# An encoder step on one core: the feed forward's input product by seven quarter products instead of eight

## The chip, the core and the metric

The kernel runs on one core of a Trainium2 chip. Its metric is the device time of one execution in microseconds (us). Five engines run their own queues, each in the order of the program: TensorE (PE in the profile, its weight loads PEld), VectorE (DVE), ScalarE (ACT), GpSimd (POOL), and SyncE (SP), which starts most transfers from memory.

## The reference

One step of a four-layer encoder for 512 prompt rows and 32 sample rows, model width 1024. Each layer has a token mixer (differential attention, mLSTM, latent attention, differential attention) and then a SwiGLU feed forward of 2816 hidden features, both behind a norm whose scale and shift come from a conditioning vector. All is computed in fp32. The part that matters here:

```python
def swiglu(h, w_in, w_out):
    a, b = jnp.split(h @ w_in, 2, axis=-1)
    return (jax.nn.silu(a) * b) @ w_out
...
        mod = (jax.nn.silu(c) @ p['w_ada'][i] + p['b_ada'][i])[:, None, :]
        sh1, sc1, gt1, sh2, sc2, gt2 = jnp.split(mod, 6, axis=-1)
...
        h = rmsnorm(x, p['g_norm2'][i]) * (1.0 + sc2) + sh2
        x = x + gt2 * swiglu(h, p['w_ffn_in'][i], p['w_ffn_out'][i])
```

## The kernel before

Activations lie transposed, 128 features to a tile and all 544 rows side by side, in two halves of 256 and 288 rows (`HALVES`). Every fp32 product is three products of a faster format: each operand is split into a high part (ScalarE's cast, `hi`) and a low part (a subtraction, `lo`), and high x high, low x high and high x low are summed in a bank of PSUM (`prod`). `split(hi, lo, src, eng)` does this; the subtraction runs on VectorE, for a few weights on GpSimd (`ON_POOL`). In the profile a weight is `raw` as loaded, `wh` and `low` when split.

The feed forward (`ffn`) has 22 column tiles `t`, each with a weight of 128x1024 for `a` and one for `b`, 8 K tiles of 128 each. For a tile, both halves of the rows are multiplied with both weights, 2 x 2 x 8 x 3 matmuls, and `glu` makes silu(a) * b (`uf`) and splits it into `uh` and `ul`. After 11 tiles an output block (`out_block`) multiplies them with the output weights, 8 output tiles in two halves, and VectorE adds each to the residual `x` (`residual`). Then come the other 11 tiles and their output block, with the squares for the next norm (`ss`, on GpSimd).

The conditioning (`mod`) of the next layers is not TensorE's work: `ada_dve` loads 128x1024 of its weights at a time (`ada`) and VectorE multiplies and sums them with the conditioning (`sc`), once for the prompt and once for the sample. It is done during the feed forwards of the first three layers, in time that VectorE has left.

`Sched` sets the order of all work ahead of time, from the author's estimate of what each instruction takes (`Engine.cost`, `Tensor._held`): an instruction takes the first free time of its engine after its operands (`hole`), work given to `later` fills the rest (`fill`), and each engine's instructions are issued in the order of the estimated times. The estimate counts each engine's time by itself. On the chip each engine then runs its queue in that order and waits where an operand is late. All recorded instructions have one line, 296 (VectorE, ScalarE, GpSimd) or 329 and 332 (TensorE), so that the rows are told apart by their tiles.

Of the kernel before, what the change touches and what calls it, by code (L numbers as in the profile page):

```python
# [8 lines left out]
F32 = mybir.dt.float32  # L9
# [6 lines left out]
P = 128  # L16
D = 1024
# [14 lines left out]
HALVES = ((0, 256), (256, T))  # L32
# [19 lines left out]
def EARLY(h, z):  # L52
    """How many of the first conditioning's tiles are made after a projection."""
    return 0 if h == 0 else 2 if z == 2 and h < 4 else 1


class Sched:
    """An order of all engines' work, from an estimate of when each instruction can run.

    Tasks are generators that issue the tensor engine's work; each yields when its next step can start: None or a  # L60
    function that gives the time. The other engines' instructions take the first free time after their operands.
    Instructions are noted first and issued by their time, a phase at once.
    """
# [49 lines left out]
    def flush(self):  # L113
        """Issues what is noted, in the order of its time."""
# [13 lines left out]
    # what is known of a tile: (first and last partition, first and last column, time)  # L128
# [42 lines left out]
    def free(self, key, bufs):  # L171
        """When a new tile of a ring can be written."""
# [3 lines left out]
    def ready(self, *aps):  # L176
        """When the tensor engine can read."""
# [9 lines left out]
    def hole(self, eng, t, cost, take=True):  # L187
        """The first free time of an engine, from t on."""
# [59 lines left out]

class Engine:
    """An engine whose instructions are noted with their time."""  # L250
# [50 lines left out]
class Tensor:  # L301
    """The tensor engine, with an estimate of how long it is held."""
# [4 lines left out]
    def _held(self, out, lhs, rhs, passes, issue, turn=False):  # L307
# [8 lines left out]
        else:  # L316
            cost = max(passes * m / 2400.0, m / 1200.0, passes * n / 2400.0) + 0.0025
# [9 lines left out]
    def matmul(self, out, lhsT, rhs, start, stop):  # L327
        self._held(out, lhsT, rhs, 1 if lhsT.dtype == F32R else 4,
                   lambda: self.pe.matmul(out, lhsT, rhs, start=start, stop=stop))  # L329
# [6 lines left out]
def tile_trunk(ctx: ExitStack, tc: tile.TileContext, I, O):  # L336
# [31 lines left out]
    class Banks:  # L368
        """PSUM banks for products and turned tiles, each use in the one that is free first.

        A bank for turned tiles is written and read before another one is asked for; one for products is shut.
        """

        def __init__(self, n):
            self.last, self.shut = [None] * n, [True] * n
# [2030 lines left out]
```

## Time and profile before

| | |
|---|---|
| median of 3 runs | 2750.12 us (2749.83 to 2750.35) |
| profiled execution | span 2748.0 us from the first to the last instruction, 2.1 us under the median; its own time outside the span isn't given |
| TensorE | busy 2705.6 us, 98% |
| VectorE | busy 1820.7 us, 66% |
| ScalarE | busy 1086.5 us, 40% |
| GpSimd | busy 238.0 us, 9% |
| mean granted TensorE clock | 0.996 of full |

Busy time is what an engine spent in instructions, waits inside an instruction with it. Shares over the span mix stages; a stage is read from a window. A matmul's duration in a row is longer than the time to the next one's start, because matmuls overlap; their rate is read from starts.

### The profile page before, as it was taken

The page shows a single profiled execution, that of the slowest core. Times are in us where ns is not written, and L with a number is a line of the kernel's source. Part 1 is how long each engine was busy: PE and PEld are TensorE (multiplying, and loading weights), DVE is VectorE, ACT ScalarE, POOL GpSimd, SP SyncE. Part 2 cuts the span into 40 slices and gives each one's busy share as a digit, 9 for nine tenths or more (in the row PEclk, how much of TensorE's full clock was granted, in tenths as well). Part 3 has the DMA queues.
Part 4 walks back from the last instruction along what each step waited for, and adds up shares of the span by engine and source line. Part 5 has one row for each costly group of instructions (what it writes and reads, how often), then busy time and mean ns, then how long its engine had stood idle before and what let it go on. Part 6 is the DMA issues. An engine that isn't in the chain of part 4 may idle for free.

```text
span 2748.0 us, 51869 instructions
## 1 busy us (share of the span) xinstructions
PE 2705.6 (98%) x21223; PEld 2590.8 (94%) x21223; DVE 1820.7 (66%) x3621; ACT 1086.5 (40%) x2382; POOL 238.0 (9%) x242
## 2 busy tenths in 40 slices
PE   9999999999999999999999999999999999999998
PEld 6888899999999999999998899999998899999998
DVE  6878777777665677777366767777558887433333
ACT  4555442122466442223255534222235554321222
POOL 1000300000200120000110020000031112000001
PEclk9999999999999999999999999999999999999999
DMA  8343244555222235455221124555333222222221
GB/s 281 129 139 123 87 153 164 187 172 180 87 83 78 76 110 174 170 183 176 80 97 33 47 78 142 170 181 177 126 108 97 77 80 75 77 88 90 88 86 68
DMA packets 101461, 330.94 MB, mean 120 GB/s; under 512 B 12840, under 2 KB 20140, under 8 KB 100840
## 3 DMA queue, kind: packets, MB, share of 16 engines
q1 hardware_dynamic: 95976, 309.48, 33.6%
q0 software_dynamic: 5248, 18.14, 1.8%
q8 instruction: 167, 2.74, 0.4%
q14 instruction: 70, 0.57, 0.1%
HBM read 314.69 MB, written 12.89 MB: 119 GB/s over the span
## 4 chain that ended last, share of the span: by engine, by line
PE 90%; DVE 6%; ACT 2%; issue 1%; DMA 0%; DVEq 0%; SPq 0%; ACTq 0%
PE mm L329 54%; PE S L329 21%; PE O L329 11%; PE T L329 2%; PE T L332 2%; DVE ht L296 1%; DVE hl L296 1%; DVE x L296 1%; ACT hh L296 1%; ACT wh L296 0%; DVE low L296 0%; DVE rq L296 0%; DVE mx L296 0%; DVE ql L296 0%; ACT rs L296 0%
## 5 line engine op out<-in xcount | busy, mean ns | idle before, releaser
L329 PE MATMUL mm<-hh,wh 128*128 128x288 f32 (+1 forms) x3078 | 909.8, 296 | 0.5 <-ACT hh L296 0.4
L329 PE MATMUL mm<-hh,low 128*128 128x288 f32 (+1 forms) x3078 | 887.9, 288 | 0.0
L329 PE MATMUL mm<-hl,wh 128*128 128x288 f32 (+1 forms) x3078 | 884.5, 287 | 2.2 <-DVE hl L296 2.2
L329 PEld LDWEIGHTS mm<-hh,wh 128*128 128x128 f32 x3078 | 580.7, 189 | 22.3 <-issue 15.1
L329 PEld LDWEIGHTS mm<-hl,wh 128*128 128x128 f32 x3078 | 581.8, 189 | 2.6 <-DVE hl L296 2.6
L329 PEld LDWEIGHTS mm<-hh,low 128*128 128x128 f32 x3078 | 581.1, 189 | 3.3 <-issue 2.4
L296 ACT CAST wh<-raw 128x1024 fp32r<-128x1024 f32 (+2 forms) x392 | 399.9, 1020 | 335.7 <-PE mm L329 159.4
L296 DVE TENSOR_TENSOR low<-raw,wh 128x1024 fp32r<-128x1024 f32 (+2 forms) x358 | 421.8, 1190 | 153.4 <-ACT wh L296 152.0
L329 PE MATMUL S<-hh,wh 128*128 128x288 f32 (+1 forms) x892 | 257.5, 289 | 0.5 <-ACT hh L296 0.5
L329 PE MATMUL S<-hl,wh 128*128 128x288 f32 (+1 forms) x892 | 256.6, 288 | 1.0 <-DVE rq L296 1.0
L329 PE MATMUL S<-hh,low 128*128 128x288 f32 (+1 forms) x892 | 257.3, 288 | 0.0
L329 PE MATMUL mm<-uh,wh 128*128 128x288 f32 (+1 forms) x836 | 241.3, 289 | 0.0
L329 PE MATMUL mm<-uh,low 128*128 128x288 f32 (+1 forms) x836 | 240.5, 288 | 0.0
L329 PE MATMUL mm<-ul,wh 128*128 128x288 f32 (+1 forms) x836 | 239.9, 287 | 0.0
L296 ACT CAST uh<-uf 128x256 fp32r<-128x256 f32 (+1 forms) x176 | 73.9, 420 | 406.1 <-DVE uf L296 405.9
L296 DVE SCALAR_TENSOR_TENSOR x<-mm,mod,x 128x256 f32<-128x256 f32 (+1 forms) x278 | 103.7, 399 | 163.3 <-PE mm L329 162.4
L296 POOL TENSOR_TENSOR ss<-ss,sq 128x256 f32<-128x256 f32 (+1 forms) x80 | 75.6, 945 | 1537.2 <-ACT sq L296 1536.9
L296 DVE CUSTOM_DVE_ANT_0 ada<-ada,sc,bada 128x1024 f32<-128x1024 f32 x152 | 194.7, 1281 | 2.6
L296 DVE CUSTOM_DVE_ANT_0 junk<-ada,sc,bada 128x1024 f32<-128x1024 f32 x152 | 194.5, 1280 | 1.0 <-DMA ada<-in_w_adaT 0.9
L329 PEld LDWEIGHTS S<-hh,wh 128*128 128x128 f32 x892 | 167.5, 188 | 2.8 <-issue 2.1
L329 PEld LDWEIGHTS S<-hl,wh 128*128 128x128 f32 x892 | 168.1, 189 | 1.8 <-DVE rq L296 1.3
L329 PEld LDWEIGHTS S<-hh,low 128*128 128x128 f32 x892 | 167.6, 188 | 0.0
(487 smaller groups left out, 5212.5 us busy)
## 6 DMA issues: line engine op xcount, KB each, us to landing
raw<-in_w_fin SPq DMA_DIRECT2D x176, 512.0 KB, 3.3
ada<-in_w_adaT SPq DMA_DIRECT2D x152, 512.0 KB, 4.5
raw<-in_w_fo SPq DMA_DIRECT2D x64, 512.0 KB, 3.3
raw<-in_w_qkv SPq DMA_DIRECT2D x45, 512.0 KB, 3.8
raw<-in_w_ada SPq DMA_DIRECT2D x24, 512.0 KB, 3.7
raw<-in_w_fl SPq DMA_DIRECT2D x32, 384.0 KB, 3.1
raw<-in_w_bh SPq DMA_DIRECT2D x24, 512.0 KB, 3.5
raw<-in_w_ao SPq DMA_DIRECT2D x16, 512.0 KB, 3.6
```

The source lines that it names most:

```text
L296: return s.work(self.kind, outs, ins, self.cost(name, args, kw, outs, ins), lambda: f(*args, **kw))
L329: lambda: self.pe.matmul(out, lhsT, rhs, start=start, stop=stop))
L332: self._held(out, in_, ident, 0, lambda: self.pe.transpose(out, in_, ident), True)
```

## The change

Both halves of the rows become 272 wide (`W`). For column tiles 2 to 21 of each layer, the weights `a` and `b` are taken as a 2 x 2 matrix of quarters (`a` and `b`, K tiles 0 to 3 and 4 to 7), the input as another (K tiles 0 to 3 and 4 to 7, first and second half of the rows), and the product is formed from seven quarter products instead of eight, with sums of quarters on both sides. Tiles 0 and 1 stay as they were (`PLAIN`).

- The weights' sums S1 to S4 are made by GpSimd (`Feed.sums`: four instructions of 128x512, one in place in `raw`, the others `st`). S1 and the second weight's right half are split as one weight; S2, S3, S4 are split apart (`Feed.quarter`, tiles `sh` and `sl`): the low part of S2 on VectorE, of S3 on GpSimd, of S4 on GpSimd for 20, 15, 15 and 0 of the 20 tiles of a layer.
- The input's sums T1 to T4 are made once a layer (`Norm.forms`).
- A tile is a task of its own (`pair_task`); results are added in PSUM, or in SBUF (`cmb`) by VectorE. The product of the two branches and both low parts `ul` are GpSimd's, for the last tile of a block VectorE's.
- There are four output blocks of 6, 6, 6 and 4 tiles, loaded in pieces; of the eight output weights 1, 4 and 6 are split by GpSimd. The last block takes all first halves before the second ones.
- Conditioning weights are loaded and summed in halves of 512 columns, 608 sums instead of 304 of twice the width.
- Three more PSUM banks serve the products in the feed forward. The estimate of a matmul's time is a little longer.

```diff
-HALVES = ((0, 256), (256, T))
+W = T // 2
+HALVES = ((0, W), (W, T))
+BLOCKS = ((0, 6), (6, 12), (12, 18), (18, 22))
+MOST = 6
+QUARTERS = 4
+OUT_ON_POOL = (1, 4, 6)
+PLAIN = 2
...
-            cost = max(passes * m / 2400.0, m / 1200.0, passes * n / 2400.0) + 0.0025
+            cost = max(passes * m / 2400.0, m / 1200.0, passes * n / 2265.0) + 0.005
...
-            for bi in range(2):
-                yield 10 * l + 2 + 2 * bi
-                for t in range(11 * bi, 11 * bi + 11):
-                    yield from (I["w_fin"][l, t, z] for z in range(2))
-                yield 10 * l + 3 + 2 * bi
-                for j in range(0, KT, 2):
-                    yield from (I["w_fo"][l, bi, j], I["w_fl"][l, bi, j // 2], I["w_fo"][l, bi, j + 1])
+            for bi, (t0, t1) in enumerate(BLOCKS):
+                yield 10 * l + 2
+                for t in range(t0, t1):
+                    for z in range(2):
+                        yield I["w_fin"][l, t, z] if t < PLAIN else (Pair(I["w_fin"][l, t, z], z, t % 4 < (4, 3, 3, 0)[l]), None)
+                yield 10 * l + 3
+                n = 1 if t1 - t0 > 4 else 2
+                for j in range(0, KT, n):
+                    yield (Pieces(l, t0, t1, range(j, j + n)), G if j in OUT_ON_POOL else V)
...
+        def sums(self, k):
+            if self.pool is None:
+                return False
+            p = self.pairs[k]
+            if not self.room():
+                return False
+            a, b = self.raws[k], self.raws[k + 1]
+            s2, s3, s4 = (sb(self.pool, [P, 512], "st", bufs=3) for _ in range(3))
+            p.update(s2=s2, s3=s3, s4=s4)
+            hi = self.hi(k, a)
+            S_.copy(hi, a)
+            G.tensor_tensor(out=s3, in0=a[:, :512], in1=b[:, :512], op=ALU.subtract)
+            G.tensor_tensor(out=b[:, :512], in0=b[:, :512], in1=b[:, 512:], op=ALU.add)
+            G.tensor_tensor(out=s2, in0=b[:, :512], in1=a[:, :512], op=ALU.subtract)
+            G.tensor_tensor(out=s4, in0=a[:, 512:], in1=s2, op=ALU.subtract)
+            lo = los[k % RAWS]
+            sub(lo, a, hi)
+            p.update(A11=(hi[:, :512], lo[:, :512]), A12=(hi[:, 512:], lo[:, 512:]))
+            return True
+
+        def second(self, k):
+            if not self.room():
+                return False
+            raw = self.raws[k + 1]
+            hi, lo = self.hi(k + 1, raw), los[(k + 1) % RAWS]
+            split(hi, lo, raw)
+            self.pairs[k].update(S1=(hi[:, :512], lo[:, :512]), A22=(hi[:, 512:], lo[:, 512:]))
+            return True
+
+        def quarter(self, k, name):
+            q = self.quarters
+            if len(q) >= QUARTERS and q[-QUARTERS] not in self.used:
+                return False
+            q.append((k, name))
+            p = self.pairs[k]
+            hi, lo = (sb(self.pool, [P, 512], t, F32R, bufs=QUARTERS) for t in ("sh", "sl"))
+            split(hi, lo, p[name.lower()], G if name == "S3" or name == "S4" and p["pool"] else V)
+            p[name] = (hi, lo)
+            return True
...
+            first = sb(pool, [P, 2], "ada1", bufs=2)
+            for c in (slice(0, D // 2), slice(D // 2, D)):
+                raw = sb(pool, [P, D // 2], "ada", bufs=3)
+                SP.dma_start(out=raw, in_=I["w_adaT"][l, t][:, c])
+                for s in range(2):
+                    yield "DVE", (raw,), 0.65
+                    V.tensor_tensor_reduce(
+                        out=junk if s == 0 else raw,
+                        in0=raw,
+                        in1=sc[:, s, c],
+                        scale=1.0,
+                        scalar=first[:, s : s + 1] if c.start else bada[:, l, t : t + 1],
+                        op0=ALU.mult,
+                        op1=ALU.add,
+                        accum_out=mods[l][:, t, s : s + 1] if c.start else first[:, s : s + 1],
+                    )
...
+        def forms(self, am, sh, tf, pf, f):
+
+            a, b = HALVES[1]
+            c = SEQ - a
+            h = KT // 2
+            tables(SILU, self.rstd(a, b))
+            for j in range(KT):
+                t = f[:, j]
+                for side, d, e in ((0, 0, c), (1, c, W)):
+                    at = stt(t[:, d:e], x[:, j, a + d : a + e], am[:, j, side : side + 1], self.rs[:, a + d : a + e], ALU.mult, ALU.mult)
+                    act(t[:, d:e], t[:, d:e], AF.Identity, bias=sh[:, j, side : side + 1])
+                split(hh[:, j, a:b], hl[:, j, a:b], t)
+                pending.discard((j, a))
+                yield lambda: at - PACE
+
+            def fold(n, k, t, eng):
+                split(tf[n][0][:, k], tf[n][1][:, k], t, eng)
+                pf.done(n, k)
+
+            for k in range(h):
+                t3, t2 = f[:, k], f[:, k + h]
+                G.tensor_tensor(out=t3, in0=t2, in1=t3, op=ALU.subtract)
+                add(t2, t3, hh[:, k, :a].bitcast(F32))
+                at = add(t2, t2, hl[:, k, :a].bitcast(F32))
+                fold("T3", k, t3, G)
+                t4 = t3
+                sub(t4, hh[:, k + h, :a].bitcast(F32), t2)
+                fold("T2", k, t2, V)
+                G.tensor_tensor(out=t4, in0=t4, in1=hl[:, k + h, :a].bitcast(F32), op=ALU.add)
+                fold("T4", k, t4, V)
+                yield lambda: at - PACE
+            yield pf.after(("plain",))
+            for k in range(h):
+                t1 = sb(nrm, [P, W], "ht", bufs=4)
+                sub(t1, hh[:, k, a:b].bitcast(F32), hh[:, k, :a].bitcast(F32))
+                add(t1, t1, hl[:, k, a:b].bitcast(F32))
+                sub(t1, t1, hl[:, k, :a].bitcast(F32))
+                split(hh[:, k, a:b], hl[:, k, a:b], t1)
+                pf.done("T1", k)
+
...
+            inputs = {n: tf[n] for n in tf}
+            inputs["T1"] = (hh[:, :h, W:], hl[:, :h, W:])
+            inputs["B22"] = (hh[:, h:, W:], hl[:, h:, W:])
+            inputs["B11"] = (hh[:, :h, :W], hl[:, :h, :W])
+            inputs["B21"] = (hh[:, h:, :W], hl[:, h:, :W])
...
+            def product(p, wn, xn, ps, start=True):
+                xs = inputs[xn]
+                yield lambda: 0.0 if wn in p else NEVER
+                w = p[wn]
+                for k in range(h):
+                    ww, xx = wk(w, k), (xs[0][:, k, :], xs[1][:, k, :])
+                    yield lambda: ready(xn, k)
+                    yield lambda: max(sched.writable(ps), sched.ready(*ww, *xx))
+                    kw = {} if start else {"skip_group_check": True}
+                    PE.matmul(ps, ww[0], xx[0], start=start and k == 0, stop=False, **kw)
+                    PE.matmul(ps, ww[1], xx[0], start=False, stop=False, **kw)
+                    PE.matmul(ps, ww[0], xx[1], start=False, stop=k == h - 1, **kw)
...
+            def eng(t):
+                return V if any(t == t1 - 1 for _, t1 in BLOCKS) else G
+
+            def part(t, i, f):
+                a, b = HALVES[i]
+                uh, ul = u[t]
+                S_.copy(uh[:, a:b], f)
+                eng(t).tensor_tensor(out=ul[:, a:b], in0=f, in1=uh[:, a:b], op=ALU.subtract)
+                pf.done("u", t, i)
...
+            def pair_task(t, p):
+                k = p["k"]
+
+                def bank():
+                    ps = yield from mm_bank()
+                    return ps, ps[:, :W]
+
+                xb, X = yield from bank()
+                yield from product(p, "A11", "B11", X)
+                s1 = sb(fp, [P, W], "cmb", bufs=6)
+                S_.copy(s1, X)
+                yb, Y = yield from bank()
+                yield from product(p, "A12", "B21", Y)
+                feed.drop_keys(k)
+                add(s1, s1, Y)
+                banks.done(yb)
+                act(s1, s1, AF.Silu)
+                yield from product(p, "S2", "T2", X, False)
+                feed.drop_keys((k, "S2"))
+                s2 = sb(fp, [P, W], "cmb", bufs=6)
+                S_.copy(s2, X)
+                gb, g = yield from bank()
+                yield from product(p, "S1", "T1", g)
+                b1 = sb(fp, [P, W], "cmb", bufs=6)
+                S_.copy(b1, g)
+                yield from product(p, "S3", "T3", X, False)
+                feed.drop_keys((k, "S3"))
+                add(b1, X, b1)
+                yield from product(p, "S4", "B22", g, False)
+                feed.drop_keys((k, "S4"))
+                add(s2, s2, g)
+                banks.done(gb)
+                last = act(s2, s2, AF.Silu)
+                eng(t).tensor_tensor(out=b1, in0=b1, in1=s2, op=ALU.mult)
+                part(t, 1, b1)
+                if t == FT - 1:
+                    tables(EXP_LN, last)
+                pf.done("late", t)
+                yield from product(p, "A22", "T4", X, False)
+                feed.drop_keys(k + 1)
+                mul(s1, X, s1)
+                banks.done(xb)
+                part(t, 0, s1)
+                live[0] -= 1
...
+                if bi < len(BLOCKS) - 1:
+                    yield from out_block(load, drop, parts, gt, mm_bank, BOTH, lead=4)
+                else:
+                    yield from out_block(load, drop, parts, gt, mm_bank, last_by_half(NBH), Norm(), finish, lead=4)
```

The engines' queues show it at three places. In GpSimd's queue of the kernel before, in the first layer, the end of the input of the feed forward (`hs`, `hl`: the sample rows) is followed directly by the squares of its last output block (`ss`):

```order
L296 TENSOR_TENSOR hs_4773<-hs_4773,rs_1002 128x256
L296 TENSOR_TENSOR hs_4773<-hs_4773,mod_97 128x256
L296 TENSOR_TENSOR hl<-hs_4773,hh 128x8x32
L296 TENSOR_TENSOR ss_5108<-ss_5108,sq_5114 128x256
L296 TENSOR_TENSOR ss_5108<-ss_5108,sq_5118 128x288
```

In the kernel after, GpSimd's queue in the second block of that feed forward, for one column tile (`st` and `raw` are sums of weights, `sl` low parts of S3 and S4, `cmb` the product of the branches, `ul` its low parts):

```order
L310 TENSOR_TENSOR sl_4979<-st_4965,sh_4978 128x512
L310 TENSOR_TENSOR sl_4984<-st_4966,sh_4983 128x512
L310 TENSOR_TENSOR st_4986<-raw_57,raw_58 128x512
L310 TENSOR_TENSOR raw_58<-raw_58 128x512
L310 TENSOR_TENSOR st_4985<-raw_58,raw_57 128x512
L310 TENSOR_TENSOR st_4987<-raw_57,st_4985 128x512
L310 TENSOR_TENSOR cmb_4982<-cmb_4982,cmb_4980 128x272
L310 TENSOR_TENSOR ul_4954<-cmb_4982,uh_4953 128x272
L310 TENSOR_TENSOR ul_4954<-cmb_4974,uh_4953 128x272
```

Nothing stood there before; these nine instructions now stand there once for each of the 20 column tiles, seven or eight of them in a block's last tile or where S4 is VectorE's.

VectorE's queue in the first layer's feed forward before, for one column tile: two low parts of weights, the branches' product and its low part for a half, the conditioning sums (`ISA`, with the read of the accumulator as an instruction of its own):

```order
L296 TENSOR_TENSOR low_68<-raw_62,wh_4813 128x1024
L296 TENSOR_TENSOR low_63<-raw_57,wh_4814 128x1024
L296 TENSOR_TENSOR uf_4818<-S_4816,silu_4817 128x256
L296 TENSOR_TENSOR ul_4755<-uf_4818,uh_4754 128x256
L296 ISA junk_4801,mod_97<-ada_4804,sc_4800,bada 128x1024
L296 ISA mod_97 128x1
L296 ISA ada_4804,mod_97<-ada_4804,sc_4800,bada 128x1024
```

And after, in a tile of the third block:

```order
L310 TENSOR_TENSOR low_66<-raw_60,wh_5175 128x1024
L310 TENSOR_TENSOR low_65<-raw_59,wh_5174 128x1024
L310 TENSOR_TENSOR sl_5177<-st_5171,sh_5176 128x512
L310 TENSOR_TENSOR cmb_5193<-mm_5183,cmb_5193 128x272
L310 ISA junk_4783,ada_1389_5190<-ada_5191,sc_4782,bada 128x512
L310 ISA ada_1389_5190 128x1
L310 TENSOR_TENSOR cmb_5189<-cmb_5189,mm_5192 128x272
L310 ISA ada_5191,ada_1389_5190<-ada_5191,sc_4782,bada 128x512
```

The two low parts stay, that of S2 (`sl`) and the sums with PSUM (`mm`) come in, and the conditioning sums are half as wide and twice as many.

TensorE's queue after, where one tile's third product ends and its fourth begins (S2 with T2, then S1 with T1, whose tile is in `hh` and `hl`):

```order
L343 MATMUL mm_5010<-T2h_4740,sh_4990 128x272
L343 MATMUL mm_5010<-T2h_4740,sl_4991 128x272
L343 MATMUL mm_5010<-T2l_4741,sh_4990 128x272
L343 MATMUL mm_5029<-hh,wh_4989 128x272
L343 MATMUL mm_5029<-hh,low_64 128x272
L343 MATMUL mm_5029<-hl,wh_4989 128x272
```

Each product is 12 such rows, a tile has seven of them, 84 rows where there were 96 of 256 or 288 columns; TensorE's whole queue has 19161 rows where it had 20122.

## Rows read from the trace of the kernel before

**Rows 1.** Page, busy us of each engine (share of the span) xinstructions

```profile
span 2748.0 us, 51869 instructions
PE 2705.6 (98%) x21223; PEld 2590.8 (94%) x21223; DVE 1820.7 (66%) x3621; ACT 1086.5 (40%) x2382; POOL 238.0 (9%) x242
```

**Rows 2.** Windows: us; PE, PEld, DVE, ACT, POOL busy (instructions); clock; DMA share, GB/s

```profile
345.00:730.00 385.00, 385.00 (x3074) 384.89 (x3074) 274.90 (x439) 112.49 (x182) 13.80 (x13) 1.00 0.48 162
412.41:484.71 72.30, 72.30 (x580) 72.30 (x579) 53.85 (x85) 19.27 (x32) 0.00 (x0) 1.00 0.49 165
```

**Rows 3.** Timeline, VectorE, steady tiles: start, us, instruction xcount, idle before

```profile
411.46 0.46 DVE L296 TENSOR_TENSOR uf<-mm,silu 128x288 f32<-128x288 f32 x1 [1.31 <-PE mm L329]
412.79 2.35 DVE L296 TENSOR_TENSOR low<-raw,wh 128x1024 fp32r<-128x1024 f32 x2
...
424.84 2.35 DVE L296 TENSOR_TENSOR low<-raw,wh 128x1024 fp32r<-128x1024 f32 x2
```

**Rows 4.** Timeline, GpSimd, 256 and 1024 columns

```profile
313.67 0.74 POOL L296 TENSOR_TENSOR ss<-ss,sq 128x256 f32<-128x256 f32 x1 [16.21 <-ACT sq L296]
...
980.80 2.39 POOL L296 TENSOR_TENSOR low<-raw,wh 128x1024 fp32r<-128x1024 f32 x1 [7.09 <-ACT wh L296]
```

**Rows 5.** Timeline, GpSimd and VectorE at three places where both work

```profile
285.25 2.37 POOL L296 TENSOR_TENSOR low<-raw,wh 128x1024 fp32r<-128x1024 f32 x1 [4.82 <-ACT wh L296]
285.33 1.26 DVE L296 SCALAR_TENSOR_TENSOR x<-mm,mod,x 128x256 f32<-128x256 f32 x3
...
691.14 1.22 DVE L296 TENSOR_TENSOR low<-raw,wh 128x1024 fp32r<-128x1024 f32 x1
691.34 1.61 POOL L296 TENSOR_TENSOR ss<-ss,sq 128x256 f32<-128x256 f32 x1 [343.11 <-ACT sq L296]
692.27 1.50 DVE L296 TENSOR_TENSOR low<-raw,wh 128x768 fp32r<-128x768 f32 x1
692.91 1.53 POOL L296 TENSOR_TENSOR ss<-ss,sq 128x288 f32<-128x288 f32 x1
...
940.44 2.39 POOL L296 TENSOR_TENSOR low<-raw,wh 128x1024 fp32r<-128x1024 f32 x1 [7.33 <-ACT wh L296]
940.50 2.34 DVE L296 TENSOR_TENSOR dd<-nd,dd 128x1 f32<-128x1 f32 x1
...
944.86 0.16 DVE L296 TENSOR_TENSOR dd<-nd,dd 128x1 f32<-128x1 f32 x1
```

**Rows 6.** Timeline, VectorE, conditioning sums and a low part of 256

```profile
408.86 1.28 DVE L296 CUSTOM_DVE_ANT_0 junk<-ada,sc,bada 128x1024 f32<-128x1024 f32 x1
410.06 0.08 DVE L296 DVE_READ_ACCUMULATOR2_ANT mod<- 128x1 f32 x1
...
418.03 0.43 DVE L296 TENSOR_TENSOR ul<-uf,uh 128x256 fp32r<-128x256 f32 x1 [0.47 <-ACT uh L296]
418.37 1.28 DVE L296 CUSTOM_DVE_ANT_0 junk<-ada,sc,bada 128x1024 f32<-128x1024 f32 x1
```

**Rows 7.** Timeline, TensorE, starts of the first and fourth layer's feed forward

```profile
342.85 0.72 PE L329 MATMUL T<-ss,ones_d 128*128 128x288 f32 x2 [3.18 <-DVE ss L296]
...
2339.49 1.30 PE L329 MATMUL T<-ss,ones_d 128*128 128x288 f32 x2 [3.19 <-DVE ss L296]
...
2341.77 0.41 PE L329 MATMUL mm<-hh,low 128*128 128x256 f32 x1
2341.98 0.41 PE L329 MATMUL mm<-hl,wh 128*128 128x256 f32 x1
```

**Rows 8.** Windows at the same two places, columns as in rows 2

```profile
340.00:344.00 4.00, 1.16 (x5) 0.98 (x6) 3.90 (x7) 2.18 (x4) 2.00 (x3) 1.00 0.17 25
2338.00:2342.00 4.00, 2.50 (x7) 1.96 (x8) 2.55 (x5) 1.91 (x5) 0.91 (x1) 0.53 0.00 0
```

**Rows 9.** Groups of ScalarE by shape: xcount, busy us, mean ns, idle before

```profile
L296 ACT CAST wh<-raw 128x1024 fp32r<-128x1024 f32 x348 | 363.7, 1045 | 292.6 <-PE mm L329 159.4 <-PE S L329 65.9 <-PE O L329 23.5
...
L296 ACT CAST uh<-uf 128x288 fp32r<-128x288 f32 x88 | 38.1, 433 | 186.6 <-DVE uf L296 186.6
```

More of the change, by code (lines that the diff above doesn't have):

```diff
@@ L396, in done @@
                     self.shut[self.last.index(t.tensor.name)] = True
-    banks = Banks(5)
+    banks = Banks((pB, f"b{i}") for i in range(5))
     def t_bank():
@@ L455, in add @@
     def add(out, a, b):
-        V.tensor_tensor(out=out, in0=a, in1=b, op=ALU.add)
+        return V.tensor_tensor(out=out, in0=a, in1=b, op=ALU.add)
     def stt(out, a, s, b, op0, op1):
@@ L529, in all_weights @@
                 continue
-            yield (w, G) if not isinstance(w, tuple) and (stage, i) in ON_POOL else w
+            if isinstance(w, tuple) and isinstance(w[0], Pair):
+                yield w[0]
+            else:
+                yield (w, G) if not isinstance(w, tuple) and (stage, i) in ON_POOL else w
             i += 1
@@ L581, in first, with room, hi, plain @@
             self.taken = n
-            return self.tiles[:]
+            return [self.tiles[k] for k in range(n)]
+        def room(self, n=1):
+            return all(len(self.his) + i < SPLITS or self.his[i - SPLITS] in self.used for i in range(n))
+        def hi(self, k, raw):
+            self.his.append(k)
+            return sb(wp, raw.shape, "wh", F32R, bufs=SPLITS)
+        def plain(self, k, eng):
+            if not self.room():
+                return False
+            raw = self.raws[k]
+            hi = self.hi(k, raw)
+            lo = los[k % RAWS][: raw.shape[0], : raw.shape[1]]
+            split(hi, lo, raw, eng)
+            self.tiles[k] = (hi, lo, k)
+            return True
@@ new lines, in load @@
+        def load(self, k):
+            ap = self.aps[k]
+            eng = V
+            if isinstance(ap, tuple):
+                ap, eng = ap
+            t = raws[k % RAWS][: ap.shape[0], : ap.shape[1]]
+            with sched.not_before(sched.let_go(t.tensor.name)):
+                for c, src in ap.parts if isinstance(ap, Pieces) else ((slice(0, t.shape[1]), ap.ap if isinstance(ap, Pair) else ap),):
+                    SP.dma_start(out=t[:, c], in_=src)
+            self.raws.append(t)
+            if isinstance(ap, Pair):
+                if ap.z == 0:
+                    self.pairs[k] = {"k": k, "pool": ap.pool}
+                else:
+                    self.steps += [(self.sums, k - 1), (self.second, k - 1)]
+                    self.steps += [(self.quarter, k - 1, n) for n in ("S2", "S3", "S4")]
+            elif eng is None:
+                self.tiles[k] = (t, None, k)
+            else:
+                self.steps.append((self.plain, k, eng))
@@ L612, in get @@
             self.more(0)
-            assert len(self.tiles) >= self.taken, "a weight that is held too long"
+            assert self.taken - 1 in self.tiles, "a weight that is held too long"
             w = self.tiles[self.taken - 1]
```

306 lines of the change are left out of this document (164 added, 142 removed).

## The prediction

> **What bounds the kernel now.** I read the page's busy table first: TensorE 98% of a span of 2748.0 us, VectorE 66%, GpSimd 9% [rows 1]. Then the stages, since that share is an average: over the first layer's feed forward and over six of its steady column tiles TensorE never stops, VectorE works three quarters of the time and GpSimd almost none [rows 2]. The period of a steady tile is read from VectorE, whose two weight splits return every 12.05 us [rows 3]. A tile issues 2 outputs x 8 K tiles x 3 products x 2 halves = 96 matmuls, so one costs 12.05/96 = 0.1255 us, half of them 256 and half 288 wide; one of 272 columns is the mean and costs the same. TensorE is the bound, and only because GpSimd and VectorE stay out of its way.
>
> **TensorE's saving.** Seven quarter products of 4 K tiles x 3 instead of eight are 84 matmuls, 10.54 us a tile. The order has 961 fewer PE rows. 20 tiles in each of 4 layers use the seven, so 80 x 12 x 0.1255 = -120.5 us. By layer the input stage is 22 x 12.05 = 265 us of TensorE before, and 2 x 12.05 + 20 x 10.54 = 235 us after. The output products stay at 8 x 2 x 22 x 3 = 1056 a layer, 132.5 us, in four blocks instead of two. Halves of 272 change no sum.
>
> **What GpSimd gets.** Its subtractions take 0.74 us for 256 columns and 2.39 for 1024 [rows 4], so by a line through both 0.77 for 272, 1.29 for 512 and 1.84 for 768. A tile gives it four sums and one or two low parts of 512, a product and two low parts of 272: 6 x 1.29 + 3 x 0.77 = 10.05 us, or 8.8 where S4 is VectorE's. That alone nearly fills the 10.54. For the input stage of a layer: 20 x 10.05, less 4 x 2.3 for the tiles that close a block, plus 16 x 0.77 for the sums of the input and the two plain tiles, 204 us in layer 0; 198 in layers 1 and 2 (five S4 fewer), 178 in layer 3 (none).
>
> **What VectorE gets beside it.** Instructions with both inputs in SBUF: two low parts of 1024 (1.14 us apart [rows 3]) and one of 512 (0.60, half of it) a tile, 2.9 us; with S4 3.5. With 4.2 us at the blocks' ends and about 24 at the start (in the order 4 x 1.14 and 60 of 32 to 272 columns, 0.33 on average, as the 0.34 of 256 [rows 6]) that is 86 us in layer 0, 89, 89 and 98. Then the conditioning sums. The order sets 156, 144 and 144 halves of 512 into the input stages of layers 0 to 2 (the other 164 into the output blocks). One of 1024 holds the engine 1.20 us [rows 6]; half of it, with a fixed part of 0.07 as in the subtractions (0.34 for 256, 1.14 for 1024), is 0.64. So 100, 92 and 92 us. ScalarE has two casts of 1.05, three of about half that and seven short ones of about 0.4 [rows 9], 6.6 us a tile, and stays hidden.
>
> **The two engines exclude each other.** This is the step on which the forecast rests. VectorE's subtraction of a 1-element column takes 0.16 us, but 2.34 when GpSimd has just begun 1024 columns, and ends as GpSimd ends [rows 5]. It holds the other way too: GpSimd's 256 columns take 1.61 instead of 0.74 behind VectorE's split. Three VectorE instructions that read PSUM and one SBUF tile run beside a GpSimd subtraction at their usual 0.4 each. So instructions with two SBUF inputs on VectorE and GpSimd's subtractions, which have them too, take turns: their times add up. Where four of them alternate, 691.14 to 694.44 [rows 5], they take 3.30 us where 1.14 + 0.74 + 0.87 + 0.80 = 3.55 would be the plain sum (the last two by the lines above), 7% less, since a fixed part overlaps.
>
> No conditioning sum ran beside GpSimd in the trace; I take it to be shut out as well, because both its tensors, the weights and the conditioning, are in SBUF, and each such pair that met GpSimd waited, whatever its operation or size. The Trainium skill says the same more generally ("SBUF — State Buffer", section "Who interferes with whom"): a VectorE instruction with two SBUF inputs contends with a GpSimd instruction that reads SBUF, and the later one waits for the whole of the other. The trace agrees for the subtractions (2.34 us against 0.16); for these sums no run here shows it, and by the page alone they would be in the sum below.
>
> **The sum.** Taking turns, the input stage costs 204 + 86 + 100 = 390 us in layer 0, 198 + 89 + 92 = 379 in layers 1 and 2, 178 + 98 = 276 in layer 3. Some of it is done in the output blocks before: ten GpSimd instructions of 512 (12.9 us) and 1.4 us of VectorE stand there in the order, three times a layer, -43 us. Such a block then holds about 34 us of turns in 36 us of matmuls, so it still fits, with its doubled residual adds (24 instructions, 7.7 us). That leaves 347, 336, 336 and 233 us, against 235 of TensorE and 265 before: +82, +71, +71, and -30 in layer 3, where TensorE stays the bound. Together +194 us. To this I add 0.5 us a tile in layers 0 to 2, +30 us. GpSimd's queue is in order, and its product and low parts behind a tile need VectorE's last product (0.46) and ScalarE's cast (0.43) [rows 3, 9] first; the next tile's sums stand behind them. On the profiled execution's 2748.0 us, which lies 2.1 under the median of the runs, this gives 2972; on the median **2975 us**.
>
> Bounds of this case: below, turns 7% cheaper in layers 0 to 2, -80, and no waits, 2865. Above, the work ahead in the output blocks worth nothing, +129, and 1 us of waits more a tile, 3135. Costed at nothing: the split conditioning loads and the weights in pieces (same bytes; DMA is half busy [rows 2]), and the borrowed banks. The start of a feed forward already holds a TensorE wait of 3.2 us [rows 7]; the new input sums lie under 24 us of plain products, and their turns are in the sum.
>
> **Rivals.**
> 1. *TensorE stays the bound and all the new work is hidden*, not slower: 2750 - 120 + 0 to 10 us, 2630 to 2640. GpSimd's 10.0 us alone would fit under 10.54, and VectorE's too. It needs the two to run side by side, against all of rows 5. It decides if the turns of a tile fall under 10.5 us. Chance 6%.
> 2. *The conditioning sums don't take turns*, only the splits do: 290, 287 and 287 less 43, so 247, 244 and 244 against 265, and -30 in layer 3: 2750 - 18 - 21 - 21 - 30 = 2660. But VectorE alone then has 2.9 + 4 x 0.37 + 7.8 x 0.72 = 10 us a tile (0.72 with the 0.08 read of the accumulator [rows 6]), and waits up to three times 1.29 behind GpSimd, which brings a tile to 12 and more and the time back to 2750, or 2790 with waits in every tile. Middle 2710. Chance 15%.
> 3. *The clock falls in the new waits*, slower still. In layer 3 TensorE waited 3.19 us; the granted clock was 0.53 in the stretch after it (the lower of its levels, 1.2 GHz), and matmuls came 0.21 us apart [rows 7, 8], instead of the 0.12 of these 256 columns. In layer 0 a wait of 3.18 left it at full [rows 7, 8]. Turns of 17 us against 10.5 of matmuls leave 6 us a tile to wait. If that comes in one piece, each tile of layers 0 to 2 loses more: at 0.09 a matmul some 20 of them, about 2 us, 60 x 2 = +120: 3095, and 3150 to 3250 with the upper bound above. The Trainium skill ("TensorE: Matmul & The Clock Gate", section on HAM oscillation) tells of a kernel that falls to the low clock at every K tile because each waits for its load. One trace row agrees (0.53 after 3.19 us) and one does not (3.18 us in layer 0); by that rule the time would be the 3095 and more given here. Chance of a time over 3135: 9%.
> 4. *The change does not do what it says*: the order shows the 961 rows gone and the sums on GpSimd; excluded.
>
> **How the numbers follow.** The likeliest case, turns with the conditioning in them, has 70% and its own range 2865 to 3135. To leave out no more than 2 in 10 the range reaches down into rival 2 and a little into rival 3: 2690 to 3150. A measurement of this kernel tells 0.2%, 5.5 us, from no change. Faster: rival 1 whole and most of rival 2, 6 + 12 = 18%. Same: 3%, out of rival 2. Slower: 79%.
>
> **What would show it.** Right: in the input stages of layers 0 to 2 a period of 16 to 18 us a tile instead of 12.05; VectorE's splits of 1024 columns well over their 1.22 us and GpSimd's of 512 over 1.29, while VectorE's instructions on PSUM stay at 0.4; TensorE waiting for the high and low parts of the sums (sh, sl, wh, low), its busy share far under 98%; layer 3 the shortest of the four, near 10.5 to 12 us a tile; output blocks still at 36 us. Wrong: splits and GpSimd's sums at their old durations with TensorE over 95% busy (rival 1), conditioning sums at half of 1.28 us beside a running GpSimd (rival 2), or matmuls 0.21 us apart through the input stages (rival 3).

## The result and the profile after

The changed kernel takes 3017.75 us (median of 4 runs, 3016.6 to 3019.76) where the kernel before takes 2749.97: ratio 1.0972, 95% interval 1.0957 to 1.0988. It is 268 us slower. The forecast was 2975, its range 2690 to 3150.

The page of the changed kernel, which answers to [rows 1] (busy us of each engine, then PE's granted clock by fortieths of the span):

```profile
span 3014.8 us, 53523 instructions
PE 2722.9 (90%) x20258; PEld 2561.5 (85%) x20258; DVE 2458.2 (82%) x4711; ACT 1335.5 (44%) x3002; POOL 1315.0 (44%) x976
PEclk9999989989999998999999998989999999899999
```

TensorE has 965 matmul rows fewer and is no longer busy all the time; VectorE went from 66 to 82%, GpSimd from 9 to 44%.

To see where, I cut both traces into feed forwards (from the first matmul of the norm's sum to the last output matmul; in layer 0 after, 324.94 to 824.54 us) and the stretches between them:

| us, layers 0, 1, 2, 3 | feed forward | mixer ahead of it |
|---|---|---|
| before | 413.7, 415.5, 413.7, 416.3 | 322.5, 239.8, 238.7, 275.2 |
| after | 499.6, 483.5, 480.8, 430.2 | 324.9, 251.3, 243.3, 288.8 |
| difference | +85.9, +68.0, +67.1, +13.9 | +2.4, +11.5, +4.6, +13.6 |

The feed forwards lost 235 us and the mixers, which the change was not to touch, 32. Inside a feed forward, windows of the changed kernel (us; PE, PEld, DVE, ACT, POOL busy with instructions; clock; DMA share, GB/s), for [rows 2]: layer 0's first six tiles (from 344.00; their first input product starts at 348.4, behind a TensorE wait of 5.4 us), its second six, the output block between them, and six of layer 3.

```profile
344.00:440.20 96.20, 74.96 (x496) 70.50 (x497) 83.31 (x137) 49.11 (x105) 63.98 (x51) 0.84 0.27 87
476.19:565.16 88.97, 72.76 (x507) 70.23 (x506) 87.39 (x133) 34.32 (x68) 69.44 (x46) 0.92 0.39 126
440.22:476.19 35.97, 35.97 (x289) 35.97 (x288) 35.03 (x71) 8.80 (x12) 15.04 (x9) 1.00 0.59 187
2716.12:2787.47 71.35, 66.51 (x507) 65.28 (x506) 39.92 (x49) 33.15 (x66) 51.76 (x38) 0.98 0.26 80
```

Six tiles hold the predicted 504 matmuls, 63.2 us of them at [rows 3]'s rate, and take 89. VectorE is the engine without a gap there (87.39 of 88.97 us), but more than a third of that is waiting inside instructions: its own work in the window is some 56 us, an estimate from 46 us of instructions with two SBUF inputs, as added up further down, and 28 short ones that read PSUM, about 0.35 us each. The timelines of VectorE and of GpSimd in that stretch show it, as [rows 5] did for splits (start, duration, instruction):

```profile
519.69 1.26 DVE L310 CUSTOM_DVE_ANT_0 ada<-ada,sc,bada 128x512 f32<-128x512 f32 x1
520.88 0.08 DVE L310 DVE_READ_ACCUMULATOR2_ANT ada<- 128x1 f32 x1
520.88 0.43 DVE L310 TENSOR_TENSOR cmb<-mm,cmb 128x272 f32<-128x272 f32 x1
521.24 1.40 DVE L310 CUSTOM_DVE_ANT_0 junk<-ada,sc,ada 128x512 f32<-128x512 f32 x1
522.57 0.08 DVE L310 DVE_READ_ACCUMULATOR2_ANT mod<- 128x1 f32 x1
522.57 0.43 DVE L310 TENSOR_TENSOR cmb<-cmb,mm 128x272 f32<-128x272 f32 x1
522.92 1.42 DVE L310 CUSTOM_DVE_ANT_0 ada<-ada,sc,ada 128x512 f32<-128x512 f32 x1
```

```profile
520.37 3.42 POOL L310 TENSOR_TENSOR sl<-st,sh 128x512 fp32r<-128x512 f32 x2
523.74 1.75 POOL L310 TENSOR_TENSOR st<-raw,raw 128x512 f32<-128x512 f32 x1
```

Each conditioning sum (CUSTOM) takes 1.26 to 1.42 us, each low part on GpSimd 1.71, where the undisturbed times are 0.74 and 1.26 (run 5 below); the additions from PSUM (cmb, mm) keep their 0.43. [rows 6] had 1.28 us for a sum of twice the width.

### The profile page after: what moved, and what is told of

Its sections match the earlier page's. It is cut to its first block, busy times and chain, and to the rows that moved or that the text cites. A ratio compares the mean times of both kernels' runs of the same rounds, so it can differ in the third digit from the quotient of the medians.

```text
span 3014.8 us, 53523 instructions
## 1 busy us (share of the span) xinstructions
PE 2722.9 (90%) x20258; PEld 2561.5 (85%) x20258; DVE 2458.2 (82%) x4711; ACT 1335.5 (44%) x3002; POOL 1315.0 (44%) x976
## 5 line engine op out<-in xcount | busy, mean ns | idle before, releaser
L343 PE MATMUL mm<-hh,wh 128*128 128x272 f32 x2694 | 813.4, 302 | 35.5 <-ACT hh L310 25.7
L343 PE MATMUL mm<-hh,low 128*128 128x272 f32 x2694 | 789.3, 293 | 12.9 <-DVE low L310 12.9
L343 PE MATMUL mm<-hl,wh 128*128 128x272 f32 x2694 | 791.0, 294 | 9.7 <-DVE hl L310 9.6
L343 PE MATMUL mm<-uh,wh 128*128 128x272 f32 x1408 | 407.7, 290 | 6.9 <-DVE x L310 6.4
L343 PE MATMUL mm<-ul,wh 128*128 128x272 f32 x1408 | 408.2, 290 | 1.6 <-DVE ul L310 1.6
L343 PE MATMUL mm<-uh,low 128*128 128x272 f32 x1408 | 406.7, 289 | 0.0
L310 POOL TENSOR_TENSOR st<-raw,raw 128x512 f32<-128x512 f32 x160 | 250.1, 1563 | 98.2 <-DMA raw<-in_w_fin 33.1
L343 PEld LDWEIGHTS mm<-uh,wh 128*128 128x128 f32 x1408 | 266.6, 189 | 8.0 <-DVE x L310 6.9
L343 PEld LDWEIGHTS mm<-ul,wh 128*128 128x128 f32 x1408 | 266.1, 189 | 2.1 <-DVE ul L310 2.0
L343 PEld LDWEIGHTS mm<-uh,low 128*128 128x128 f32 x1408 | 266.5, 189 | 0.2
```

The lines of the kernel that those rows point to most:

```text
L310: return s.work(self.kind, outs, ins, self.cost(name, args, kw, outs, ins), lambda: f(*args, **kw))
```

## The experiments

Theory: instructions with two SBUF inputs on VectorE and GpSimd's take turns, and this sum of turns is the new bound of layers 0 to 2. First rival: VectorE is simply overloaded. Second: conditioning only fills gaps. The mixers' 32 us had no theory yet.

**1. S3 and S4 on VectorE.** One line of `quarter`:

```diff
-            split(hi, lo, p[name.lower()], G if name == "S3" or name == "S4" and p["pool"] else V)
+            split(hi, lo, p[name.lower()], V)
```

> The changed kernel with the low parts of S3 and S4 (130 of 512 columns, 110 of them in layers 0 to 2) all on VectorE; everything else as it is. Turn-taking (both engines share one order of turns): each move swaps a turn of about 1.29 us on GpSimd for one of about 0.60 on VectorE, so 130 x 0.69 = -90 us: 2928, between 2900 and 2960, and VectorE stays near 98% busy in the stages of layers 0 to 2 with fewer microseconds in each instruction. Rival, VectorE's own load is the bound there (98% busy) and GpSimd only runs beside it: 110 x 0.60 = +66 us more on the bound: 3084, between 3065 and 3100.

Measured: 2981.22 us, 36 less than the change, above the expected range. VectorE got 110 x 0.60 = 66 us more of its own work in layers 0 to 2, and their feed forwards still came out 23.5 us shorter together (494.9, 472.9 and 472.6), so overload falls. The blocks of six tiles went from 87 to 90 us to 81.5 to 82.2 in layers 0 to 2: 5.3 to 8.1 us less, where 10.5 to 12 moves a block make 7.2 to 8.3 by the theory. That agreement is in part luck: the planner also put fewer conditioning sums into these blocks, 33 instead of 43 in layer 0's second (477.99 to 560.17), 6.7 us less at 0.67 each. VectorE's own work in that block hardly changed, and the turns, added up as further down, fell by 15 us, the block by 7. In layer 3 the blocks went from 71.4 and 72.5 to 64.3 and 65.0. In all, the input blocks gained 76 us, and 41 were given back: 33 in the last output blocks of layers 0 to 2 and 8 in the mixers. Windows of this kernel (layer 0's second block and its last output block, and six tiles of layer 3):

```profile
477.99:560.17 82.18, 67.42 (x508) 65.44 (x506) 79.78 (x124) 35.46 (x68) 47.88 (x35) 0.98 0.39 122
769.36:824.08 54.72, 33.41 (x197) 30.85 (x196) 52.66 (x138) 10.21 (x19) 4.99 (x6) 0.72 0.51 162
2698.41:2762.69 64.28, 64.11 (x507) 63.66 (x506) 44.50 (x54) 33.49 (x66) 42.82 (x33) 1.00 0.30 89
```

The program, which knows nothing of turns, puts conditioning that found no gap ahead of the last output block (`fill(True)`). VectorE is full there, and the block took 54.7 us instead of 35.2. Layer 3 has no conditioning, and TensorE became its bound.

**2. No conditioning sums.** A constant stands in for the later layers' conditioning.

```diff
+            if queue:
+                V.memset(mods[l + 1], 0.1)
...
+                queue = []
             yield from ffn(l, after_ffn, queue, keep)
```

> The changed kernel without the conditioning sums and their loads (the conditioning of the later layers is a constant, so the output is not the reference's). Turn-taking with the conditioning in it: the stages of layers 0 to 2 fall from 87 to 90 us to about layer 3's 71 to 73, and a little more where S4 is GpSimd's; their feed forwards from 500, 484 and 481 us to 435 to 450: about -140, so 2878, between 2850 and 2910, and GpSimd's sums of 512 columns fall from 1.57 us towards 1.3. Rival, the conditioning only fills time in which VectorE waits, and the weight sums and splits alone make the loss: 3005 to 3018.

Measured: 2817.99 us, 200 less. Feed forwards 422.9, 425.8, 425.1 and 428.5; blocks of six 69.3 to 70.0 in layers 0 to 2; GpSimd's sums of two raw weights 1.375 us instead of 1.563. Layer 0's second block (columns as above):

```profile
468.12:537.54 69.42, 65.67 (x508) 63.92 (x507) 35.63 (x44) 34.14 (x67) 57.27 (x44) 1.00 0.28 82
```

The second rival falls. The time lies under the expected range: layers 0 to 2 came out a little under layer 3's 428.5, where 435 to 450 was expected. It also shows what stays: without any conditioning the change is still 2.4% slower than before (interval 1.0225 to 1.0255).

**3. Two sources of the mixers' 32 us, each alone on the kernel before.**

```diff
-HALVES = ((0, 256), (256, T))
+W = T // 2
+HALVES = ((0, W), (W, T))
```

> The kernel before with halves of 272 columns instead of 256 and 288, and nothing else of the change. Of the 32 us that the stages outside the feed forwards lost, the refitted estimate alone gave back 13.1 in layer 3's attention, but only 1.8 of the 11.5 in the mLSTM. If the halves make the mLSTM's loss (tiles of 128 rows now straddle their edge): 2760 to 2775. If the loss comes with the feed forward before it: 2747 to 2755.

Measured: 2761.07 us, ratio 1.0040 (1.0027 to 1.0053), but not in the mixers (323.7, 240.9, 238.1, 276.5): 8.2 of the 10 us lie in the first feed forward, most of them in its last output block. The time fell into the range given for the mLSTM, but the mLSTM lost only 1.1 us: the expectation named the wrong place.

```diff
-            cost = max(passes * m / 2400.0, m / 1200.0, passes * n / 2400.0) + 0.0025
+            cost = max(passes * m / 2400.0, m / 1200.0, passes * n / 2265.0) + 0.005
```

> The kernel before with the refitted estimate of a matmul (columns / 2265 + 0.005 instead of / 2400 + 0.0025), and nothing else of the change. It changes only the order in which instructions are written. If it is the cause of the 32 us outside the feed forwards: 2770 to 2785. If not: 2745 to 2755.

Measured: 2777.1 us, ratio 1.0095 (1.0080 to 1.0110). Mixers 325.8, 241.7, 239.6 and 288.4: layer 3's attention alone lost 13.2 of the 13.6 us, by the order of instructions and nothing else. How its rows stand differently there was not followed further.

**4. The changed kernel with the old estimate**, the same line the other way.

> The changed kernel with the old estimate of a matmul (columns / 2400 + 0.0025). If the estimate costs the same on both kernels (26 us on the kernel before): 2992, between 2985 and 3002. Rival, the new feed forward needs the refitted estimate to be ordered well, and what the mixers gain is lost there: 3010 to 3040.

Measured: 2968.95 us, 49 less, nearly twice what was expected: 18 in the mixers (324.5, 247.4, 240.6, 277.6) and 29 in the feed forwards (492.5, 478.0, 478.1, 416.4). The rival falls; the refitted estimate made the new feed forward worse too.

**5. The conditioning vector in PSUM.** The sharpest test of turns: the same sums, once with both inputs in SBUF, once with one in a PSUM bank.

```diff
+            if l and at != (s, c):
+                S_.copy(by, sc[:, s, c])
+                at = s, c
...
-                in1=sc[:, s, c],
+                in1=by if l else sc[:, s, c],
```

> Control for the next run: the changed kernel with the conditioning sums of the next layer made in four passes over its 48 tiles (one half of the columns, one sample each), so each weight half is loaded twice, and seven PSUM banks for products instead of eight. Both inputs of a sum stay in SBUF. The number of sums and of turns is the same: 3018, between 3005 and 3040; a sum beside GpSimd still takes 1.1 to 1.2 us on average.

> As the control, but the conditioning vector of each pass lies in the eighth PSUM bank, so a sum reads one SBUF and one PSUM input. Turn-taking between instructions with two SBUF inputs: a sum no longer takes a turn, its mean falls from about 1.15 to 0.65 us, VectorE has 11 us of work a tile of its own, and the blocks of six tiles in layers 0 to 2 fall from 87 to 90 us to 70 to 78: 2875, between 2840 and 2930. Rival, a sum is held up whatever its second input is, or VectorE's own load is the bound: within 15 us of the control.

Measured: control 3129.4 us, with PSUM 3043.1, 86 less. The groups of conditioning sums, control first (count, then min/median/max in ns, first and last start):

```profile
L310 DVE CUSTOM_DVE_ANT_0 ada<-ada,sc,bada x296: 732/903/1965, 405.2 to 2333.6; 128x512 f32<-128x512 f32 x148
L310 DVE CUSTOM_DVE_ANT_0 ada<-ada,sc,ada x296: 732/752/2716, 407.1 to 2409.9; 128x512 f32<-128x512 f32 x148
```

```profile
L310 DVE CUSTOM_DVE_ANT_0 ada<-ada,by,bada x288: 728/742/751, 462.8 to 2243.9; 128x512 f32<-128x512 f32 x144
L310 DVE CUSTOM_DVE_ANT_0 ada<-ada,by,ada x288: 731/746/752, 573.4 to 2306.9; 128x512 f32<-128x512 f32 x144
```

And VectorE's and GpSimd's timelines with PSUM, where both work:

```profile
510.94 0.74 DVE L310 CUSTOM_DVE_ANT_0 ada<-ada,by,bada 128x512 f32<-128x512 f32 x1
511.61 0.08 DVE L310 DVE_READ_ACCUMULATOR2_ANT ada<- 128x1 f32 x1
511.61 0.43 DVE L310 TENSOR_TENSOR cmb<-mm,cmb 128x272 f32<-128x272 f32 x1
511.96 0.73 DVE L310 CUSTOM_DVE_ANT_0 ada<-ada,by,bada 128x512 f32<-128x512 f32 x1
```

```profile
511.61 2.52 POOL L310 TENSOR_TENSOR sl<-st,sh 128x512 fp32r<-128x512 f32 x2
```

Two low parts on GpSimd take 1.26 us each while the sums beside them keep their 0.74. Not one of 576 sums with a PSUM input waited: the longest took 752 ns, the shortest 728. With SBUF inputs they reach 2716. The same six tiles, control first (columns as above):

```profile
478.33:560.15 81.82, 69.73 (x507) 67.18 (x506) 73.25 (x107) 34.56 (x68) 66.98 (x45) 0.96 0.53 167
```

```profile
478.30:549.62 71.32, 65.62 (x508) 63.88 (x506) 55.35 (x101) 34.80 (x68) 59.60 (x45) 1.00 0.60 189
```

71.3 us for 81.8 (with 28 conditioning sums in the window for 30), near the 69.4 without conditioning. So the turns are shown, with the conditioning in them, and both rivals fall. Both totals missed their ranges (3005 to 3040, 2840 to 2930), and both kernels are slower than the change as it was, for a reason of my own making: in passes over all 48 tiles, with each weight loaded twice, the conditioning ended late, and the next layer's first matmuls waited for it. TensorE's waits with PSUM (total us, times, longest):

```profile
PE mm L343 <- ACT hh L310: 99.6, 34, 39.5
PE mm L343 <- DVE low L310: 83.4, 5, 39.5
PE mm L343 <- ACT cmb L310: 59.6, 50, 3.1
```

**6. Four plain tiles at the start**, for the input's sums to hide under.

```diff
-PLAIN = 2
+PLAIN = 4
...
-                    yield from plain_pairs(range(PLAIN))
+                    for t in range(0, PLAIN, 2):
+                        yield from plain_pairs(range(t, t + 2))
...
```

> The changed kernel with the first four column tiles of a feed forward by plain products instead of two, so that the sums of its input have 48 us of plain matmuls to hide under. Layer 3's first block took 108.0 us with the change; 18 us of norm as before, two plain tiles at 12.05 and four at 10.54 are 84, so some 22 us a layer stand there beside the sums of the input. If those sums are the cause: 12 to 18 us less in each layer's first block, 2945 to 2975 in all. Rival, the start waits for the norm itself: layer 3 gains nothing and pays 3 us for the two more plain tiles, the others gain up to 6 (12.05 for 14.8 us a tile): 2998 to 3020.

Measured: 2972.84 us, 45 less. First blocks 99.7, 104.1, 101.4 and 95.8 us instead of 115.3, 114.5, 114.6 and 108.0. The stall is in this window of the changed kernel, layer 3's start:

```profile
2625.00:2640.00 15.00, 8.52 (x28) 6.50 (x28) 14.73 (x20) 5.60 (x11) 9.19 (x9) 0.50 0.00 0
```

28 matmuls in 15 us, with VectorE full (14.73 us), mostly of the input's sums, taking turns with GpSimd; the granted clock is at its lower level (1.2 GHz) in all of it, having fallen just ahead, while TensorE waited 2.8 us. The rival falls: layer 3 gained 12.2 us. Part of the stall may be the clock's: 47 matmuls ran at that level (2622.3 to 2642.1), 0.23 us apart where nothing was waited for instead of 0.1255, some 5 us by this estimate.

**7. Towards a version that beats both.** The combined one takes the old estimate, four plain tiles, every S4 on VectorE, and conditioning by quarters from PSUM, each weight loaded once:

```diff
+                for s in range(2):
+                    S_.copy(by[:, s * n : s * n + n], sc[:, s, c * n : c * n + n])
+                for l, t in rest[g : g + 12 : 2]:
...
+                            one(r, by[:, s * n : s * n + n], a, b, r if s else junk[:, :n])
```

> A version against both kernels: old estimate, four plain tiles, every S4 on VectorE, and the conditioning by quarters of 256 columns with the vector in a PSUM bank (12 tiles to a pass, each weight loaded once), which left no long wait at a layer's end. If the terms add: 2818 without any conditioning, 49 less by the old estimate, some 40 less at the starts, and 10 to 40 more for conditioning beside GpSimd: 2740 to 2770, no more than a tie with the kernel before. Rival, VectorE with 11 to 12 us a tile of its own becomes the bound in layers 0 to 2: 2800 to 2880.

Measured: 2889.67 us, above both ranges. Blocks of six take 66.7 to 69.9, so the conditioning's turns no longer set them; but conditioning was left over again, and five waits for the residual (`x`) behind it cost TensorE 134.1 us. VectorE's own load is the bound now, as the rival said, and it shows at the layers' ends.

The two-bank version makes the sums in halves of 512 from two PSUM banks:

```diff
-            banks.lend([(pO, "O"), (pF, "f0")])
+            banks.lend([(pO, "O")])
...
+                for s in range(2):
+                    S_.copy(by[s], sc[:, s, c])
```

> As the combined version, but the conditioning in halves of 512 columns with both samples' vectors in two PSUM banks (six banks left for products), so 192 sums of about 0.74 us a layer, 143 us of VectorE, instead of 384 of about 0.56 with the read of the accumulator, 215 us. In the combined version TensorE lost 134 us in five waits for the residual behind conditioning that was left over at the end of layers 0 to 2. If that was VectorE's sheer load, most of the 134 goes: 2755 to 2785. Rival, six banks are too few for two tiles in flight and the blocks of six grow from 67 to 70 us to 75 and more: 2800 to 2860.

Measured: 2829.43 us, above the expected range and inside the rival's, but not for the rival's reason: six tiles take 67.4, so six banks are enough. The waits for `x` fell from 134.1 to 47.4 us (total us, times, longest; combined version first):

```profile
PE mm L343 <- DVE x L310: 134.1, 5, 56.7
```

```profile
PE mm L343 <- DVE x L310: 47.4, 16, 7.5
```

```diff
-                if l == 0:
-                    queue = [(0, t) for t in range(40, 48)] + queue
```

(with these eight tiles added to the 24 of the first mixer, and the places of all 32 among its weights, `EARLY`, set anew)

> The two-bank version with the eight conditioning tiles of layer 0's own gate made by TensorE in the first mixer, as 24 others are already, instead of by VectorE at the start of layer 0's feed forward. That takes 32 sums, 24 us, from VectorE, which is the bound there (67 of 70 us busy in a block of six), and adds some 0.7 us a tile of TensorE (an estimate of the kernel's planner: eight products of 0.073 us and a turn), 6 us. If VectorE's load is what keeps layer 0's feed forward at 450 us beside 432 and 429 in the next two, it falls to 430 to 434 and the time to 2810 to 2820. If not: 2829 to 2838.

Measured: 2809.15 us, a little under the expected range; layer 0's feed forward 429.5 instead of 450.3, the mixer ahead of it 329.0 instead of 323.9.

```diff
-OUT_ON_POOL = (1, 4, 6)
+OUT_ON_POOL = tuple(range(8))
```

> As the run before, and all low parts of the output weights on GpSimd instead of three of eight. Five of 768 columns a block of output, about 0.9 us each, leave VectorE: 16 us a layer. In the output blocks GpSimd works 9 to 16 of 36 us, and the conditioning takes no turns any more, so 5 x 1.84 us more fit. If VectorE's load is the bound in layers 0 to 2, the 12 to 25 us that TensorE waits at their last output blocks and the next mixers' starts shrink by 16 a layer: 2760 to 2785, still not under the kernel before. Rival, these low parts come late and the output blocks grow past 36 us: 2820 to 2860.

Measured: 2749.52 us (median of 11 runs) beside 2751.32 for the kernel before: ratio 0.9994 (0.9985 to 1.0003). Better than expected, 268 us under the change, and a tie with the kernel before. Feed forwards 414.3, 416.6, 416.2 and 405.0, mixers 330.7, 241.8, 239.5 and 277.9. Its page (as above):

```profile
PE 2649.4 (96%) x20497; PEld 2510.1 (91%) x20497; DVE 2140.3 (78%) x4613; ACT 1362.1 (49%) x3022; POOL 1218.1 (44%) x946
```

No version tried beats the kernel before by more than the measurement tells.

## Why the prediction came out as it did

- **TensorE's saving** (-120.5): the matmuls are gone as counted, 504 in six tiles. It was not collected in the change: the nearest is layer 3 with S3 on VectorE (run 1), 64.3 us for the 63.2.
- **The two engines exclude each other**, conditioning included: right, and shown by run 5. In the window of six tiles (476.19 to 565.16) the turns at undisturbed durations are 30 GpSimd instructions of 512 by 1.29, 15 of 272 by 0.77 (three in each of five tiles; the last tile of a block has none, so that GpSimd has five or six instructions there and not the seven or eight said ahead) and one of 768 by 1.84, 52 us, and VectorE's 43 sums by 0.67 (from start to the accumulator's read in run 5), ten low parts by 1.14, three of 768 by 0.86, five by 0.60 and a product by 0.35, 46 us: 98 in 89 us, so about 10% overlaps where the prediction had 7% [rows 5]. The overlap is not constant: counted the same way, the same six tiles have 88 us in the control's 81.8 and 83 in run 1's 82.2. With the conditioning in PSUM (68 in 71.3) or left out (67 in 69.4) the turns no longer add up to the time, and TensorE is busy 65.6 and 65.7 us of it.
- **The Trainium skill** ("SBUF — State Buffer", section "Who interferes with whom") was cited for two SBUF inputs. The Trainium skill also says there that a VectorE instruction with at most one SBUF input, outside its two-port modes, does not contend with GpSimd; run 5 agrees (752 ns at most against 2716).
- **The sum by layer**: +82, +71 and +71 predicted, +85.9, +68.0 and +67.1 measured. The layers' sum is right, its place in them less so: later blocks of six ran at 14.5 to 15.0 us a tile instead of the 16 to 18 forecast, and the starts were dearer (first blocks of 115 us; less 16 for the startup of before, worked out as for layer 3 below, and two plain tiles, 18.7 us for each of the four others); that the two met is luck. The separate +30 for waits was not needed: layers 0 to 2 lost 221 us, not 254.
- **Layer 3, -30**: wrong, +13.9. TensorE did not stay its bound. "The new input sums lie under 24 us of plain products" failed: the first block took 108.0 us, where the startup of before (19: 151.5 us to the first output product less 11 x 12.05), two plain tiles and four of 10.54 make 85, and run 6 took back 12.2. And its blocks took 71.4 and 72.5 for 63.2 of matmuls. With S3's low part on VectorE (run 1) they took 64.3 and 65.0; but with the same work on every engine and the old estimate (run 4) they took 66.75 each, so that 4.6 and 5.7 of the 8.2 and 9.3 us came with the order of instructions (the first of the two, columns as above):

```profile
2681.34:2748.09 66.75, 64.91 (x507) 63.79 (x506) 39.73 (x49) 33.83 (x67) 51.51 (x38) 1.00 0.29 86
```

The turns' total does not explain the blocks: it is 62.1 us worked out as above, and run 2's layers 0 to 2, with S4 still on GpSimd, have 67 and took 69.4, where its layer 3 took 71.3. That S3's low part comes late in GpSimd's queue would fit run 1, and is not shown.
- **What was left out of the sum**: the refitted estimate was never priced. It costs 26 us on the kernel before and 49 on the changed one, 18 of the mixers' 32 there and 14 in layer 3's feed forward (430.2 to 416.4 in run 4). "Halves of 272 change no sum" was wrong by 10 us on the kernel before. Of the mixers' other 14 us, 7.6 are layer 1's; some of it is conditioning left over from layer 0 (251.3 us with it, 244.4 without), the rest is open.
- **Output blocks at 36 us**: right for those of six tiles; layer 0's last one, of four tiles, took 35.2 where layer 3's took 24.9.
- **Rivals**: the first and second fell (98 us of turns in six tiles are 16 us a tile, not under 10.5; the conditioning sums do take turns, run 5). Of the third, the granted clock did fall, 0.84 and 0.92 in stages where the prediction had full, and no run separates the clock's share: at 0.92 VectorE was without gaps (87.39 of 88.97 us), at 0.84, in the first block, it was not (83.31 of 96.20).

The mechanism was right; that the total came within 43 us is in part luck, because three errors met: layers 0 to 2 came out 33 us less than the sum with its waits, layer 3 44 more, the mixers 32 more.

## What to carry to other kernels

Before moving work from TensorE to "idle" GpSimd, add up the GpSimd instructions and VectorE's with two SBUF inputs as if they were one engine, stage by stage. The cheapest way out was to lay one input in PSUM: it took the conditioning out of the turns at next to no cost in its own duration (a median of 742 to 746 ns, beside 732 at the least in SBUF). It pays in the total only if that work still ends in time, as runs 5 and 7 show. And price a refitted scheduling estimate by itself: one raised by 8% (from 0.116 to 0.125 us for a matmul of 272 columns) was worth 1 to 1.6% here.

## What the runs showed of the hardware

- A custom multiply-and-sum waits for GpSimd like a subtraction does, and stops waiting when its second input comes from PSUM (728 to 752 ns over 576 sums; GpSimd beside some of them at its undisturbed 1.26 to 1.29 us).
- Where the engines alternate, a sum of 512 and a GpSimd subtraction of 512 take about 1.70 us a pair (starts 521.24 and 522.92), not 0.67 + 1.29 = 1.96, with an addition from PSUM on VectorE in between: part of GpSimd's work overlaps with that, or with the other's turn.
- Taking work from the less loaded of two excluding engines and giving it to the busier one made the kernel 36 us faster (run 1). The same subtraction takes 0.60 us on VectorE and 1.29 on GpSimd; how much of the 36 us that explains is not shown, since conditioning sums moved out of the blocks as well.
